# A hybrid encoder layer on one core: new order tables for TensorE, ScalarE, VectorE and GpSimd

## The chip, the core and the metric

The kernel runs on one core of one Trainium2 chip. The metric is the device time of one execution in microseconds (us), lower is better. Several executions are timed and their median is taken. One further execution is recorded by the hardware profiler, and all durations below come from that one.

In the rows, PE is TensorE (matmuls; PEld is its weight load), DVE is VectorE, ACT is ScalarE, POOL is GpSimd, and SP is SyncE. The letter q behind an engine means its queue: SPq rows are the DMAs that SP issues.

## What is computed

One layer of a streaming encoder, on 1024 prompt rows and 64 sample rows with a cache of 512 positions, all in fp32:

```python
def mixer_and_mlp(x):                      # x: (1024 + 64, 1024)
    z = x @ w_in                           # q, k, v and gate of FoX; u, v of the SGU; q, k, v of stick-breaking
    o_fox = softmax(q_f @ k_f.T / 8 + c_t - c_s) @ v_f        # 6 heads x 64, causal
    o_sgu = gelu(u) * (tril(w_s) @ layer_norm(gelu(v)) + b_s) # chunks of 128 positions, 4 groups x 64
    o_sb  = stick_breaking(q_s, k_s) @ v_s                    # 6 heads x 64, strictly causal
    o = rms_norm_per_head(concat(o_fox, o_sgu, o_sb)) * g_mix
    x = layer_norm(ALPHA * x + o @ w_out)
    h = relu(x @ w_up) ** 2                                   # 1024 -> 4096
    return layer_norm(ALPHA * x + h @ w_down)                 # 4096 -> 1024
```

The new rows of k, v, the forget gates and the SGU's v are outputs too.

## The kernel before

**Stages.** Everything is written once in Python, in a natural order, and then reordered. The mixer takes the first 600 us of the profiled execution: loads and transposes of x, the projections of k, v and q (`tok_mm`, L620 to L640), FoX, stick-breaking, the SGU's v and u (`sgu_v` L1052, `sgu_u` L1122), and the output product with its layer norm (`mix`, L483, and L440 to L530). Then comes `up` until about 958 us, `down` until 1295.3 us and a last layer norm of 10.5 us (the tail).

**Exactness.** A product of fp32 is made from three passes of a high and a low part (`PASSES`): for each operand ACT writes the high part and DVE or POOL the low part (`lo_sub`, L349 when the helper records it).

**Gelu in the SGU.** For each of nine row tiles t, `sgu_u` adds two halves of the product (tile `up`, L1137, DVE) and calls `gelu` (L1032): ACT squares into a tile `g1u` (L1033), DVE multiplies (L1034), ACT takes a sigmoid (L1035), POOL multiplies into a tile `sguu` (L1036), and SP stores `sguu` to DRAM (`u_dr`, L1143). `g1u` and `sguu` share one ring of three buffers (`tag="gl", bufs=3`). A tile that takes over the buffer of an earlier `sguu` has to wait until the store has read it. Which tile takes over from which is not written in the code: the pool hands out buffers in the order in which the ordered program frees them.

**The output mix** reads `o` back from DRAM (tiles `oo`), squares it on ACT (`sq`, L448), scales it on DVE (L455), transposes it on PE (`op`, L463), writes the result as high and low part (`oTb`, ACT L465 and DVE L349) and multiplies on PE into `mx` (L507). `ptssb`, `pthssb`, `ossb`, `ptnsb`, `ptnnsb` and `osbsb` are the last transposes, weights and outputs of the stick-breaking attention on the sample rows, which run beside it.

**Up.** The 4096 columns come in 16 pairs p. Each product of a 2 x 2 block is made with seven products of sums (`Chain`, L1572): a chain for s=0 (288 columns) and one for s=1 (256) each use four PSUM banks `zA`, `zB`, `zC`, `zD`, and a product is 12 matmuls (4 steps of depth by 3 passes, L1591). `zA` holds three products in turn; after each, ACT copies it out (`sn`, `sn`, `hh`, L1602), and the next product in that bank waits for the copy. The weights of pair p are loaded as `wr`; ACT and POOL make `wa` of them (L1529, L349), DVE makes sums in place (`w_sums`, L1538 to L1542), and ACT and DVE make `ws` of those (L1812, L349). DVE adds the products to `hh` (L1605 to L1611), squares the relu (L1623) and makes sums (L1632 to L1635); SP stores those (L1636 to L1640).

**Down.** `Down` (L2025) walks over groups g of 256 rows of h with accumulators A, B and D. The operands `h4a`, `h4b` and the weight parts `wd`, `b` are split the same way: ACT writes high parts (L1529, L1750), and `st` copies (L1754) help DVE to make low parts (L1755). The load buffers `hx`, `hr` and `awa` (DMAs at L1740, weights and accumulators at L1705 and L1766) are shared by several loads in turn.

**What sets the order.** Behind the body, `_build` takes the traced instructions of each engine and a table `ORDER[engine]` (L49 on). A word `n+k` means: n times, take the k-th of those that are left (0 is the next one as traced). Each instruction is tied to the one before it on its engine, so every engine runs exactly its table's order:

```python
        for word in ORDER[eng].split():
            n, k = (int(x or d) for x, d in zip(re.match(r"(\d*)\+?(\d*)", word).groups(), (1, 0)))
            for _ in range(n):
                i = left.pop(k)
                if prev is not None:
                    tc.add_manual_dep(i, prev.name, mybir.DependencyInfo(
```

The engines work their queues strictly in order, and waits between engines follow from the data. The table of SP orders all its DMAs.

Of the kernel before, what the change touches and what calls it, by code (L numbers as in the profile page):

```python
# [2446 lines left out]
```

## Time and profile before

| | before |
|---|---|
| median of 3 executions | 1312.68 us (1309.43 to 1313.89) |
| the profiled execution | 1307.53 us |
| its span (first to last instruction) | 1305.8 us |
| granted TensorE clock | 0.998 |
| PE busy | 1282.4 us, 98% of the span, 8851 matmuls |
| DVE, ACT, POOL busy | 958.9, 723.6, 609.3 us |

The profiled execution lies 5.2 us below the median and 1.9 us below the lowest of the timed ones. A row of the timeline reads: start, duration, engine, source line, operation, output and inputs, tile shape, count of equal instructions in a row, and in brackets how long the engine had been idle before it and what ended the idle time.

### The profile page before, as it was taken

The numbers are of one execution on the slowest core, as the hardware profiler recorded it, in microseconds if no ns is written. First come the engines' busy times: TensorE is split into PE (matmuls) and PEld (weight loads), VectorE is DVE, ScalarE is ACT, GpSimd is POOL, SyncE is SP. The second block draws the span as 40 slices with busy tenths as digits, with TensorE's granted clock in tenths as the row PEclk, the third lists the DMA queues.
The fourth block names the chain that finished last, engine by engine and source line by source line (L and its number), as shares of the span: only waits on it lengthen the run. The fifth ranks groups of instructions, "written<-read, shape, count | busy, mean of one in ns | idle before, by whom it ended". The sixth has DMA issues, their size and how long they took to land.

```text
span 1305.8 us, 24299 instructions
## 1 busy us (share of the span) xinstructions
PE 1282.4 (98%) x8851; PEld 1184.5 (91%) x8851; DVE 958.9 (73%) x1800; ACT 723.6 (55%) x1560; POOL 609.3 (47%) x670
## 2 busy tenths in 40 slices
PE   9999999999999999999999999999999999999996
PEld 9999999999989997878999999999988888888885
DVE  4678676677896587798877576766797767677777
ACT  4467666677675574343533222322368677667775
POOL 2232222356775576866322212121188666565557
PEclk9999999999999999999999999999999999999999
DMA  7445574232313358341333434434577344434433
GB/s 235 118 137 159 180 212 118 77 80 57 98 30 89 97 189 278 100 145 61 125 121 128 162 131 145 167 123 157 188 256 265 128 157 147 148 125 149 144 126 133
DMA packets 158048, 185.64 MB, mean 142 GB/s; under 512 B 27740, under 2 KB 116124, under 8 KB 157928
## 3 DMA queue, kind: packets, MB, share of 16 engines
q1 hardware_dynamic: 155832, 183.01, 43.6%
q8 instruction: 70, 1.15, 0.4%
q10 hardware_dynamic: 2096, 1.07, 0.3%
q14 instruction: 50, 0.41, 0.1%
HBM read 117.65 MB, written 60.10 MB: 136 GB/s over the span
## 4 chain that ended last, share of the span: by engine, by line
PE 47%; DVE 2%; DMA 1%; issue 0%; ACT 0%; SPq 0%; POOL 0%; DVEq 0%; ACTq 0%; POOLq 0%
PE A L2056 13%; PE zA L1591 10%; PE zD L1591 7%; PE D L2056 6%; PE zC L1591 3%; PE zB L1591 3%; PE B L2056 3%; PE ds L2102 1%; PE ds L2100 1%; PE lastD L2056 1%; DMA rd<-w_down 1%; PE lastB L2056 0%; DMA h_dr<-y 0%; DVE hh L1623 0%; DVE acc L2168 0%
## 5 line engine op out<-in xcount | busy, mean ns | idle before, releaser
L349 POOL TENSOR_TENSOR wa<-wr,wa 128x512 fp32r<-128x512 f32 x41 | 60.0, 1487 | 223.6 <-ACT wa L1529 223.4
L349 POOL TENSOR_TENSOR wd<-rd,wd 128x512 fp32r<-128x512 f32 x77 | 104.0, 1359 | 106.5 <-ACT wd L1529 105.2
L1591 PE MATMUL zD<-xo,ws 128*128 128x256 f32 (+1 forms) x720 | 141.9, 287 | 0.0
L1591 PE MATMUL zA<-xo,ws 128*128 128x288 f32 (+1 forms) x720 | 131.7, 288 | 1.1 <-ACT sn L1602 1.1
L1591 PEld LDWEIGHTS zD<-xo,ws 128*128 128x128 f32 x720 | 111.2, 188 | 0.2
L1591 PEld LDWEIGHTS zA<-xo,ws 128*128 128x128 f32 x720 | 107.2, 188 | 1.6 <-ACT sn L1602 1.6
L507 PE MATMUL mx<-xT,oTb 128*128 128x512 f32 (+1 forms) x416 | 107.3, 406 | 0.8 <-DVE y L512 0.8
L1602 ACT ACTIVATE sn<-zA 128x256 f32<-128x256 f32 (+1 forms) x80 | 31.1, 393 | 131.0 <-PE zA L1591 115.7
L635 PE MATMUL kvfox<-wkvfox,xT 128*128 128x256 f32 (+3 forms) x624 | 100.2, 294 | 0.8 <-ACT wkvfox L608 0.7
L635 PE MATMUL kvsb<-wkvsb,xT 128*128 128x256 f32 (+1 forms) x624 | 100.7, 291 | 0.0
L2056 PE MATMUL A<-wd,wd 128*128 128x512 f32 x312 | 93.6, 390 | 0.0
L507 PEld LDWEIGHTS mx<-xT,oTb 128*128 128x128 f32 (+1 forms) x416 | 74.0, 186 | 17.5 <-DVE y L512 1.0
L635 PEld LDWEIGHTS kvfox<-wkvfox,xT 128*128 128x128 f32 (+1 forms) x624 | 84.5, 187 | 1.6 <-ACT wkvfox L608 0.9
L635 PEld LDWEIGHTS kvsb<-wkvsb,xT 128*128 128x128 f32 (+1 forms) x624 | 84.6, 187 | 0.0
L1591 PE MATMUL zB<-xo,wa 128*128 128x288 f32 (+1 forms) x360 | 83.3, 287 | 0.0
L1591 PE MATMUL zC<-xo,wa 128*128 128x288 f32 (+1 forms) x360 | 82.4, 288 | 0.0
L1723 POOL TENSOR_TENSOR rd<-rd 128x512 f32<-128x512 f32 x56 | 74.3, 1327 | 13.2 <-DVE b L349 10.4
L821 POOL TENSOR_TENSOR sgsb<-sgsb,snsb 128x255 f32<-128x255 f32 (+7 forms) x48 | 58.2, 1213 | 45.2 <-DVE snsb L819 39.3
L2056 PE MATMUL A<-wd,h4a 128*128 128x512 f32 x240 | 77.4, 390 | 0.0
L1529 ACT ACTIVATE wd<-rd 128x512 fp32r<-128x512 f32 x105 | 63.3, 621 | 22.1 <-DMA rd<-w_down 10.2
L2023 DVE TENSOR_TENSOR acc<-acc,A 128x512 f32<-128x512 f32 x73 | 49.5, 683 | 29.8 <-PE A L2056 29.4
L819 DVE TENSOR_TENSOR_SCAN snsb<-snsb,one 128x256 f32<-128x256 f32 (+7 forms) x48 | 68.3, 1425 | 4.0 <-ACT snsb L818 3.2
(560 smaller groups left out, 3946.2 us busy)
## 6 DMA issues: line engine op xcount, KB each, us to landing
h_dr<-hh SPq DMA_DIRECT2D x30, 512.0 KB, 3.2
rd<-w_down SPq DMA_DIRECT2D x30, 512.0 KB, 4.4
wr<-w_up SPq DMA_DIRECT2D x13, 1024.0 KB, 5.8
hr<-h_dr SPq DMA_DIRECT2D x31, 384.0 KB, 3.1
h_dr<-hh SPq DMA_DIRECT2D x30, 384.0 KB, 3.9
raw<-w_in SPq DMA_DIRECT2D x44, 256.0 KB, 3.2
wo_dr<-swo SPq DMA_DIRECT2D x32, 256.0 KB, 2.3
xT<-wo_dr SPq DMA_DIRECT2D x8, 1024.0 KB, 8.0
```

The lines of the kernel that those rows point to most:

```text
L349: eng.tensor_tensor(out, src, hi.bitcast(F32), op=ALU.subtract)
L507: nc.tensor.matmul(acc[0:m], oT[:, k, hx, 0:m], wo[k // 4][hw][:, k % 4, cs], start=(i == 0), stop=(i == len(seq) - 1))
L635: nc.tensor.matmul(acc[0:n, c0:c0 + n1 - n0], xT[k // 4][:, k % 4, c:c + n], wt[:, k, hw, n0:n1], start=(i == 0), stop=(i == len(seq) - 1))
L819: nc.vector.tensor_tensor_scan(g[:, 0:n][:, ::-1], g[:, 0:n][:, ::-1], one.broadcast_to([P, n]), 1.0, op0=ALU.mult, op1=ALU.bypass)
L821: nc.gpsimd.tensor_tensor(s[:, 0:n - 1], s[:, 0:n - 1], g[:, 1:n], op=ALU.mult)
L1529: nc.scalar.activation(hi, raw, AF.Copy)
L1591: nc.tensor.matmul(z, w[:, hw, k], xop(s, bo, hx)[:, k, :], start=(new and k == 0 and j == 0), stop=(k == 3 and j == 2), skip_group_check= ...
L1602: nc.scalar.activation(c, z, AF.Copy)
L1723: eng.tensor_tensor(r[:, o], r[:, x], r[:, y], op=ALU.subtract)
L2023: nc.vector.tensor_tensor(out, out if other is None else other, bank, op=ALU.add)
L2056: nc.tensor.matmul(z, h[:, hx, q, o], wset[self.c % 2][q][:, hw, wb], start=((n in (0, 3) or n == 1 and self.c == 0) and q == 0 and j == 0 ...
L2100: nc.tensor.matmul(z, hs[:, q, f].rearrange("p h c -> p (h c)"), w[:, 0], start=(q == 0 and f == 0), stop=False, skip_group_check=True)
```

## The change

Only the four tables `ORDER["PE"]`, `ORDER["ACT"]`, `ORDER["DVE"]` and `ORDER["POOL"]` are new. `ORDER["SP"]`, every line of code and every instruction are as before: 8851 matmuls on PE, and the same 1502, 1701 and 656 ordered instructions on ACT, DVE and POOL. The author's planner, which wrote the tables, took a DMA's landing time from the bytes that are outstanding when it is issued, and was made to keep the products of one accumulator of `up` together. The tables take 40 lines less in all, so a line of code has a number that is 40 lower after the change: L1033 is L993, L349 is L309.

```diff
 ORDER["ACT"] = """
-3 +3 2+5 1 +1 1 2+3 +4 +2 +7 +3 +6 +2 +6 1 +9 2+1 +3 3 +3 +4 +8 1 +1 +2 +5 2 +2 2+6 5 2+5 1 +2 +3 1 2+12 +1 +3
+2 +7 +4 +6 4 2+3 2+4 +2 +6 +2 1 +4 1 +4 1 +7 +3 3 +6 +5 +3 +7 +2 2 +4 1 +7 1 +6 +1 4 +5 +1 +2 1 +3 2+13 +1 +4
...
```

Most instructions move by some 10 to 30 places. Three places follow. `[waits ...]` names what an instruction waits for: an engine's semaphore, or a DMA's (DMAHW and a number).

**The opening of the output mix, ACT.** Here the last gelus of the SGU's u (`g1u6`, `g1u7`: row tiles 6 and 7) run among the last pieces of the stick-breaking attention of the sample rows. Before:

```order
L851 ACTIVATE pthsb2_3_1_3_7822<-ptsb2_3_1_3_7818 128x384 [waits DVE_49,PE_49]
L1035 ACTIVATE g1u6_7710<-g1u6_7710 128x256 [waits DVE_49]
L448 ACTIVATE sq1_7616<-oo1_1_7614 128x512 [waits DMAHW2_49,Activation_49,Pool_49]
L851 ACTIVATE pthssb2_7849<-ptssb2_7844 128x512 [waits PE_49]
L906 ACTIVATE osbsb2_3_1_7837<-osb2_3_1_7725 128x256 [waits PE_49]
L1033 ACTIVATE g1u7_7757<-up6_7261 128x256 [waits Pool_49]
L851 ACTIVATE ptnnsb2_7854<-ptnsb2_7852 128x128 [waits DVE_49]
L1035 ACTIVATE g1u7_7757<-g1u7_7757 128x256 [waits DVE_49]
```

After:

```order
L811 ACTIVATE pthsb2_3_1_3_7822<-ptsb2_3_1_3_7818 128x384 [waits PE_49,Activation_49]
L993 ACTIVATE g1u6_7710<-up6_7261 128x256 [waits DMAHW4_49]
L408 ACTIVATE sq1_7616<-oo1_1_7614 128x512 [waits DVE_49,DMAHW2_49,Activation_49,Pool_49]
L995 ACTIVATE g1u6_7710<-g1u6_7710 128x256 [waits DVE_49]
L811 ACTIVATE pthssb2_7849<-ptssb2_7844 128x512 [waits PE_49]
L993 ACTIVATE g1u7_7757<-up6_7261 128x256 [waits DMAHW1_49,Pool_49]
L811 ACTIVATE ptnnsb2_7854<-ptnsb2_7852 128x128 [waits Activation_49]
L995 ACTIVATE g1u7_7757<-g1u7_7757 128x256 [waits DVE_49]
L866 ACTIVATE osbsb2_3_1_7837<-osb2_3_1_7725 128x256
```

`g1u7` moved ahead of `osbsb2_3_1`, and `ptnnsb2` stays behind it. Its wait changed too: it took over a buffer from `g1u6` before, and takes over that of `sguu5` now, so it waits for the store of `sguu5` (DMAHW1 in this row). `g1u6` in the same way now waits for a store, that of `sguu4`.

On DVE at the same place, before:

```order
L349 TENSOR_TENSOR pthssb2_7849<-ptssb2_7844,pthssb2_7849 128x512 [waits Activation_49]
L455 TENSOR_TENSOR oo1_0_7613<-oo1_0_7613,ss1_7618 128x512 [waits DMAHW1_49,Pool_49]
L1034 SCALAR_TENSOR_TENSOR g1u7_7757<-g1u7_7757,up6_7261 128x256 [waits Activation_49]
L349 TENSOR_TENSOR ptnnsb2_7854<-ptnsb2_7852,ptnnsb2_7854 128x128 [waits PE_49,Activation_49]
L450 TENSOR_REDUCE ss1_7618<-sq1_7616 128x8
L1034 SCALAR_TENSOR_TENSOR g1u8_7775<-g1u8_7775,up8_7292 64x256 [waits DMAHW4_49,DMAHW3_49,Activation_49]
L451 SCALAR_TENSOR_TENSOR ss1_7618<-ss1_7618,rge_7590 128x8 [waits DVE_49]
```

After:

```order
L309 TENSOR_TENSOR ptnnsb2_7854<-ptnsb2_7852,ptnnsb2_7854 128x128 [waits DVE_49,PE_49,Activation_49]
L411 SCALAR_TENSOR_TENSOR ss1_7618<-ss1_7618,rge_7590 128x8 [waits DVE_49]
L994 SCALAR_TENSOR_TENSOR g1u7_7757<-g1u7_7757,up6_7261 128x256 [waits DMAHW1_49,Pool_49]
L415 TENSOR_TENSOR oo1_0_7613<-oo1_0_7613,ss1_7618 128x512 [waits Pool_49]
L309 TENSOR_TENSOR pthssb2_7849<-ptssb2_7844,pthssb2_7849 128x512 [waits PE_49]
L875 TENSOR_REDUCE otsb2_3_0_7734<-otpsb2_3_0_7735 128x2x64 [waits DMAHW5_49]
```

`ptnnsb2` and `g1u7`, which need ACT's results of the same names, moved ahead of `oo1_0` (the next tile of the mix) and of `pthssb2`.

**Up, p=8.** ACT copies out `zA8_0` and `zA8_1` and makes `ws9`. Before:

```order
L1529 ACTIVATE wa9_10778<-wr9_10776 128x512 x2
L1602 ACTIVATE sn8_0_10793<-zA8_0_10797 128x288 [waits DVE_49,PE_49,Activation_49]
L1602 ACTIVATE sn8_0_10793<-zA8_0_10797 128x288 [waits PE_49]
L1602 ACTIVATE sn8_1_10795<-zA8_1_10811 128x256 [waits DVE_49,PE_49,Activation_49]
L1812 ACTIVATE ws9_10789<-wr9_10776 128x1024 [waits DVE_49] x2
L1602 ACTIVATE sn8_1_10795<-zA8_1_10811 128x256 [waits PE_49]
L1602 ACTIVATE hh8_0_10794<-zA8_0_10797 128x288 [waits DMAHW2_49,DMAHW1_49,DMAHW3_49,DVE_49,PE_49]
L1602 ACTIVATE sn8_1_10795<-zA8_1_10811 128x256 [waits PE_49]
```

After:

```order
L1489 ACTIVATE wa9_10778<-wr9_10776 128x512 x2
L1562 ACTIVATE sn8_0_10793<-zA8_0_10797 128x288 [waits DVE_49,PE_49,Activation_49]
L1562 ACTIVATE sn8_1_10795<-zA8_1_10811 128x256 [waits DVE_49,Activation_49]
L1772 ACTIVATE ws9_10789<-wr9_10776 128x1024 [waits DVE_49,PE_49]
L1772 ACTIVATE ws9_10789<-wr9_10776 128x1024
L1562 ACTIVATE sn8_0_10793<-zA8_0_10797 128x288 [waits PE_49]
L1562 ACTIVATE sn8_1_10795<-zA8_1_10811 128x256
L1562 ACTIVATE hh8_0_10794<-zA8_0_10797 128x288 [waits DMAHW2_49,DMAHW1_49,DMAHW3_49,DVE_49,PE_49]
L1562 ACTIVATE sn8_1_10795<-zA8_1_10811 128x256 [waits PE_49]
```

The two halves of `ws9` now stand ahead of the second copies of both banks, where they stood between or behind them. On DVE, between the sums of `wr9` that `ws9` needs, before:

```order
L1538 TENSOR_TENSOR wr9_10776<-wr9_10776 128x4x128 [waits DMAHW0_49,Pool_49]
L1539 TENSOR_TENSOR wr9_10776<-wr9_10776 128x4x128 [waits DVE_49]
L1632 TENSOR_TENSOR hh7_0_10568<-hh7_0_10568 128x256
L1541 TENSOR_TENSOR wr9_10776<-wr9_10776 128x4x128 [waits DVE_49]
L1623 SCALAR_TENSOR_TENSOR hh7_1_10570<-hh7_1_10570 128x1024
L1542 TENSOR_TENSOR wr9_10776<-wr9_10776 128x4x128 [waits DVE_49]
```

After:

```order
L1498 TENSOR_TENSOR wr9_10776<-wr9_10776 128x4x128 [waits DMAHW0_49,Activation_49,Pool_49]
L1595 TENSOR_TENSOR hh7_0_10568<-hh7_0_10568 128x256 [waits DVE_49]
L1583 SCALAR_TENSOR_TENSOR hh7_1_10570<-hh7_1_10570 128x1024 [waits DVE_49]
L1592 TENSOR_TENSOR hh7_0_10568<-hh7_0_10568 128x256
L1593 TENSOR_TENSOR hh7_0_10568<-hh7_0_10568 128x256 [waits DVE_49]
L1499 TENSOR_TENSOR wr9_10776<-wr9_10776 128x4x128
L1592 TENSOR_TENSOR hh7_1_10570<-hh7_1_10570 128x256
L1501 TENSOR_TENSOR wr9_10776<-wr9_10776 128x4x128 [waits DVE_49,Activation_49]
L1593 TENSOR_TENSOR hh7_1_10570<-hh7_1_10570 128x256 [waits DVE_49]
L1502 TENSOR_TENSOR wr9_10776<-wr9_10776 128x4x128 [waits DVE_49]
```

Four more instructions on `hh7` stand between the first and the last sum than before. On PE the third product of `zA8_0`, which needs the second copy, has 37 more matmuls ahead of it (11 of `zA8_1`, 9 of `zD8_0`, 7 each of `zB8_0` and `zD8_1`, 5 of `zB8_1`, less 2 of `zC8_0`), and all products stand in runs of up to 12.

**Down, group 1, ACT.** `h4b` is the operand that PE's first products of the group need; its second half comes from the load buffer `awa`, which held weights before (`wd0_1<-awa`). Before:

```order
L2073 ACTIVATE p10_0_12654<-A0_0_12640 128x512 [waits PE_49]
L1529 ACTIVATE wd0_1_12494<-awa_12374 128x512 [waits DVE_49]
L2073 ACTIVATE p10_1_12656<-A0_1_12647 128x512 [waits PE_49]
L1750 ACTIVATE h4b_12629<-hx_12375 128x512 [waits DMAHW5_49]
L1754 ACTIVATE st9_12712<-h4b_12629 128x512 [waits DVE_49,Activation_49]
L1750 ACTIVATE h4a_12369<-hx_12375 128x512 [waits PE_49]
L1754 ACTIVATE st11_12769<-h4a_12369 128x512 [waits DVE_49,Activation_49]
L1529 ACTIVATE b12_1_12628<-rb0_1_12839 128x512 [waits DMAHW0_49]
L1529 ACTIVATE b12_0_12626<-rb0_0_12835 128x512 [waits DMAHW7_49]
L1529 ACTIVATE wd1_0_12625<-rd1_0_12733 128x512 [waits DMAHW3_49,Pool_49]
L1750 ACTIVATE h4b_12629<-awa_12374 128x512 [waits DMAHW2_49]
```

After:

```order
L1489 ACTIVATE wd0_0_12493<-rd0_0_12296 128x512
L1710 ACTIVATE h4b_12629<-hx_12375 128x512 [waits DMAHW5_49]
L1489 ACTIVATE wd0_1_12494<-awa_12374 128x512
L1710 ACTIVATE h4a_12369<-hx_12375 128x512 [waits PE_49]
L1489 ACTIVATE b12_0_12626<-rb0_0_12835 128x512 [waits DMAHW7_49]
L1714 ACTIVATE st9_12712<-h4b_12629 128x512 [waits DVE_49,Activation_49]
L1714 ACTIVATE st11_12769<-h4a_12369 128x512 [waits DVE_49]
L1489 ACTIVATE b12_1_12628<-rb0_1_12839 128x512 [waits DMAHW0_49]
L1710 ACTIVATE wd0_0_12493<-hr1_0_12693 128x384 [waits DMAHW6_49,PE_49]
L1710 ACTIVATE h4b_12629<-awa_12374 128x512 [waits DMAHW2_49]
L1714 ACTIVATE st10_12752<-h4b_12629 128x512 [waits Activation_49]
L1489 ACTIVATE wd1_0_12625<-rd1_0_12733 128x512 [waits DMAHW3_49,Pool_49]
```

The second half of `h4b` now stands ahead of `wd1_0<-rd1_0` instead of behind it. The last `wd0_1<-awa`, after which the buffer can be loaded again, moved from ahead of the first half of `h4b` to behind it.

414 rows, old and new, of the table ORDER are left out of this document.

## The prediction

> **What bounds the kernel now.** I read the page's busy times first, then the waits of PE, then the timeline at the places where PE waits or where the new tables change what stands ahead of what.
>
> ```profile
> span 1305.8 us, 24299 instructions
> PE 1282.4 (98%) x8851; PEld 1184.5 (91%) x8851; DVE 958.9 (73%) x1800; ACT 723.6 (55%) x1560; POOL 609.3 (47%) x670
> ```
>
> PE is busy in all but 23.4 us of the span, and the same 8851 matmuls run in either order. The waits of PE, longest first, and PE's last row:
>
> ```profile
> PE warm L1370 <- POOL ident masks.py:199: 1.6, 1, 1.6
> PE zA L1591 <- ACT sn L1602: 1.1, 2, 0.6
> PE otpfox L914 <- DVE kpfox L349: 0.9, 1, 0.9
> PE mx L507 <- DVE y L512: 0.8, 1, 0.8
> ...
> PE A L2056 <- ACT h4b L1750: 0.7, 1, 0.7
> ...
> PE sgu L635 <- DVE up L1137: 0.5, 1, 0.5
> ```
>
> ```profile
> 1293.77 1.52 PE L2056 MATMUL A<-wd,wd 128*128 128x512 f32 x6
> ```
>
> PE ends at 1295.3 and the span at 1305.8, so 10.5 of the 23.4 us are the tail behind PE, 1.6 are the start, and 11.3 are small waits, none above 0.9. That is all a reordering of PE's suppliers can win. What it can lose has no such limit: each engine runs its queue strictly in order, and PE can't make up a wait later.
>
> **Part one, what goes.** In up, PE waits twice behind ACT:
>
> ```profile
> 651.84 0.38 ACT L1602 ACTIVATE sn<-zA 128x256 f32<-128x256 f32 x1 [2.35 <-DMA h_dr<-y]
> 652.28 0.62 PE L1591 MATMUL zA<-xo,ws 128*128 128x256 f32 x3 [0.59 <-ACT sn L1602]
> ```
>
> ```profile
> 759.09 1.06 ACT L1812 ACTIVATE ws<-wr 128x1024 fp32r<-128x1024 f32 x1 [0.87 <-DVE wr L1542]
> 760.05 0.67 ACT L1602 ACTIVATE sn<-zA 128x288 f32<-128x288 f32 x2
> 760.50 0.40 PE L1591 MATMUL zA<-xo,ws 128*128 128x288 f32 x1 [0.56 <-ACT sn L1602]
> ```
>
> In the new PE table the products that wait here start later by over 1 us of PE work, so both waits go: -1.2. In FoX the wait of `otpfox` goes, since DVE's work on `kpfox` stands earlier: -0.9. At the end of the SGU's u the wait of `sgu` for `up` goes (0.5), and two of `osb` behind it get 0.1 later each: -0.3. `mx` for `y` gets 0.1 us more room against a wait of 0.8: -0.1. In the tail two pieces of VectorE work of the last layer norm move ahead of PE's last evacuations; I take -0.5, between 0 and the 1.4 of two pieces of 128x512 (0.68 each at 509.94 below). Keeping the products of one accumulator together saves nothing that I can read: runs of one accumulator step at the same pace as mixed rows.
>
> ```profile
> 793.86 0.86 PE L1591 MATMUL zA<-xo,wa 128*128 128x256 f32 x6
> 756.60 1.61 PE L1591 MATMUL zA<-xo,ws 128*128 128x288 f32 x11
> ```
>
> A lone matmul's row shows about 0.28 us, so the runs step at (0.86 - 0.28) / 5 = 0.116 and (1.61 - 0.29) / 10 = 0.132 us; I take -0.3 for fewer changes, between 0 and -1. Sum of what goes: -3.3.
>
> **Part two, the mix opening.** Before, the stores of `sguu` hold POOL, and nobody waits for that:
>
> ```profile
> 503.55 0.32 SPq L1143 DMA_DIRECT2D u_dr<-sguu  x1
> 513.17 0.73 POOL L1036 TENSOR_TENSOR sguu<-g1u,up 128x256 f32<-128x256 f32 x1 [1.95 <-DMA u_dr<-sguu]
> ```
>
> ```profile
> 500.89 0.42 DVE L1034 SCALAR_TENSOR_TENSOR g1u<-g1u,up 128x256 f32<-128x256 f32 x1
> 505.16 0.67 DVE L450 TENSOR_REDUCE ss<-sq 128x8 f32<-128x512 f32 x1
> 509.94 0.68 DVE L455 TENSOR_TENSOR oo<-oo,ss 128x512 f32<-128x512 f32 x1
> 511.25 0.42 ACT L1033 ACTIVATE g1u<-up 128x256 f32<-128x256 f32 x1 [1.68 <-POOL sguu L1036]
> 511.58 0.26 ACT L851 ACTIVATE ptnnsb<-ptnsb 128x128 fp32r<-128x128 f32 x1
> 511.39 0.27 PE L463 MATMUL op<-ident,oo 128*128 128x128 f32 x1
> 508.96 2.00 PE L507 MATMUL mx<-xT,oTb 128*128 128x512 f32 x8
> ```
>
> The store of `sguu5` is issued at 503.55, and the tile that takes over its buffer starts at 513.17: 9.6 us. After the change ACT's `g1u7` takes over that buffer. The store itself comes later: DVE's `g1u5` stood at 500.89 and now stands behind the low part of `oTb`, whose successor started at 505.16, so that is its earliest time; from `g1u5` to the issue took 2.66 us, so the issue moves to 507.8. If the store lands when the queue clears, as before at 513.2, `g1u7` starts then, `ptnnsb` 0.33 later (511.25 to 511.58), DVE's part of it 0.46 behind that, then the sums and `g1u7` (0.65) and `oo1_0` (0.68): 515.3. PE needs `oo1_0` for the transposes that ran at 511.39. Its new table has 14 matmuls of 512 columns more ahead of them and one of 256 less, at (2.00 - 0.40) / 7 = 0.229 and 0.11 us each: 3.1, so at 514.5. PE waits 0.8, and 0.6 more for `pthssb`, which DVE now makes behind `oo1_0`: 1.4. If the store takes 9.6 us from its new issue, all is 4.2 later: 5.6. If it takes as little as the 2.1 us below, nothing waits: 0.
>
> ```profile
> uu<-u_dr SPq DMA_DIRECT2D x3, 128.0 KB, 2.1
> ```
>
> I take +2.8, the middle between the ends: the store joins the same loads as before, but later. The Trainium skill, DMA: Bandwidth & Descriptors, section "Anatomy of one DMA — SWDGE (gpsimd) path", puts a DMA at about 2.0 us and 1 us per 436 KB, which for 128 KB would be an estimate of 2.3 us: by that rule this term is 0. The trace disagrees here with 9.6 us, though the quiet row of 2.1 us agrees.
>
> **Part three, up at p=8.** After the change both halves of `ws9` stand on ACT ahead of the second copy of `zA8_0`, which is the order that cost PE 0.56 at 760.50 in p=6.
>
> ```profile
> 795.32 0.68 DVE L1538 TENSOR_TENSOR wr<-wr 128x512 f32<-128x512 f32 x1
> 798.72 0.68 DVE L1542 TENSOR_TENSOR wr<-wr 128x512 f32<-128x512 f32 x1
> 799.65 0.75 DVE L1633 TENSOR_TENSOR hh<-hh 128x256 f32<-128x256 f32 x2
> 799.43 1.06 ACT L1812 ACTIVATE ws<-wr 128x1024 fp32r<-128x1024 f32 x1 [0.60 <-DVE wr L1542]
> 798.35 1.02 PE L1591 MATMUL zA<-xo,ws 128*128 128x288 f32 x7
> ```
>
> The last sum ended at 799.4. Four more pieces of `hh` of 0.35 to 0.42 stand ahead of it: 800.9. Two halves of `ws9` at 1.0 and the copy at 0.4 end at 803.3. PE's third product began at 798.35; 37 more matmuls stand ahead (23 of 0.116, 14 of 0.132): 4.5, so 802.85. PE waits 0.5. The same order in p=7 makes `ws8` and so the load of `wr9` up to 1.5 later, and then it is 2.0. I take +1.5, and for p=7, 9 and 15, whose tables mix `ws`, `sn` and `hh` alike, +0.5 each (the 0.56 of p=6), between 0 and 3 together.
>
> **Part four, down's group 1.** Before, ACT waits for a weight load, and behind it stands `h4b`:
>
> ```profile
> 963.11 0.62 ACT L1529 ACTIVATE wd<-awa 128x512 fp32r<-128x512 f32 x1
> 964.04 4.11 POOL L349 TENSOR_TENSOR wd<-awa,wd 128x512 fp32r<-128x512 f32 x2
> 963.79 0.32 SPq L1740 DMA_DIRECT2D hx<-h_dr  x1
> 968.95 0.63 ACT L1750 ACTIVATE h4b<-hx 128x512 fp32r<-128x512 f32 x1 [4.00 <-DMA hx<-h_dr]
> 970.19 0.38 SPq L1740 DMA_DIRECT2D awa<-h_dr  x1
> 977.26 0.63 ACT L1529 ACTIVATE wd<-rd 128x512 fp32r<-128x512 f32 x1 [1.40 <-DMA rd<-w_down]
> 977.79 0.61 ACT L1750 ACTIVATE h4b<-awa 128x512 fp32r<-128x512 f32 x1
> 978.46 0.50 PE L2056 MATMUL A<-wd,h4b 128*128 128x512 f32 x1 [0.71 <-ACT h4b L1750]
> ```
>
> The change takes `h4b` from behind that load, but puts the last reader of `awa` behind the wait for `hx`: it runs at 969.5 instead of 963.11, POOL's half takes 1.3 to 2.05 behind it, so the load of `awa` is issued at 971.5 to 972.2 instead of 970.19. With the 5.1 us of `hx` (963.79 to 968.95) it lands at 976.6 to 977.3, and `h4b` is ready at 977.2 to 977.9. PE wants it at 977.5 (0.2 earlier than before): a wait of 0 to 0.4 in place of 0.7. If DVE's new order holds the load of `hx` as well, as its work on `wd0_1` now stands up to 1.2 later, the wait is 1.6. Net -0.7 to +0.9; I take +0.8, because `h4a` and the first accumulators wait in the same chain.
>
> **Part five, the rest.** The stretch of the SGU's v is the tightest for DVE, and the new table loads ACT and DVE in it a little later:
>
> ```profile
> 340.00:400.00 60.00, 57.57 (x465) 54.88 (x464) 53.70 (x101) 40.86 (x102) 48.18 (x54) 1.00 0.19 47
> ```
>
> DVE is busy 53.7 of 60 us there. I take +0.5 (0 to 1), +0.2 for the head, whose first split waits for a later load, and +0.5 for the later groups of down, where no row shows a wait now (0 to 2). Sum of what comes: 2.8 + 1.5 + 1.5 + 0.8 + 0.5 + 0.2 + 0.5 = 7.8. Net 7.8 - 3.3 = +4.5 us, from 1307.5 to 1312.0 in a profiled execution. The median of the timed executions lies 5.2 above the profiled one, so 1312.7 + 4.5 = 1317.2. I can tell about 0.3%, 3.9 us, from no change.
>
> **The rivals.** First, not slower but faster: the new landings are right, the store of `sguu5` lands within 3 us, and the waits of parts three to five stay below 0.1 as before. Then only what goes counts, with the 0.7 of `h4b`: -4.0, 1308.7. For it: the quiet 2.1 us, and no row of before shows PE late in p=8. Against it: 9.6 us at that very place. It decides at a landing of 511.8, 1.4 us ahead of before's. By the page's 2.3 us alone, with the other parts as forecast, the time would be 1314.4. Second, no difference: half of the new waits fall on slack (the store at its lower 1.4, p=8 at 0.5, the rest at half), +3.6 against -3.3: 1313.0. For it speaks that PE is 98% busy and each place moves by tenths. Third, worse: the store takes its 9.6 us and the late loads of up and down all take their upper ends (5.6 + 2.0 + 3 + 0.9 + 3.2): 14.7 - 3.3, 1324.1.
>
> **How the numbers follow.** Forecast 45%, no difference 28%, faster 20%, worse 7%. The forecast's own range is 1314 to 1321; two in three of its cases lie beyond 3.9 us, which with the worst makes slower 0.38. The faster rival lies just beyond the bound: 0.20. The rest, 0.42, is no difference, so slower and same are nearly even, and the sign of the forecast is not sure. The range runs from 1308 (the faster rival) to 1324 (the worst).
>
> **What would show it.** In the profile after: no wait of `zA` near 651 and 760; ACT's `g1u` of row tile 7 idle for a DMA `u_dr<-sguu`, and `op` on PE released late by DVE's `oo` near 513; `zA` waiting for `sn` near 802; `A` for `h4b` near 977, with ACT released by the DMA of `awa` instead of `rd`. It is wrong if `g1u` starts before 512 or if PE's waits sum to less than before's.

## The result, and the profile after

The kernel after takes 1304.28 us in the median (6 runs, 1302.47 to 1307.09), the one before 1311.37 beside it (6 runs, 1309.43 to 1313.89). The ratio is 0.9945 with a 95% interval of 0.9929 to 0.9961: faster by 0.55%. Forecast were 1317.2.

The head of the page after (span; busy time of each engine, its share of the span, its instructions), and then PE's waits (what PE did next and in which line, what ended the wait; us in total, times, the longest):

```profile
span 1303.0 us, 24347 instructions
PE 1276.9 (98%) x8851; PEld 1180.1 (91%) x8851; DVE 964.4 (74%) x1800; ACT 721.5 (55%) x1560; POOL 606.2 (47%) x670
```

```profile
PE sgv L595 <- DVE sgvv L996: 1.5, 3, 1.0
PE sgm L1043 <- ACT so L1047: 1.2, 1, 1.2
PE mx L467 <- ACT oTb L425: 1.2, 1, 1.2
PE zA L1551 <- ACT sn L1562: 1.1, 3, 0.5
PE Ssb L795 <- ACT snsb L778: 1.1, 2, 0.7
PE zD L1551 <- DVE hh L1565: 0.9, 2, 0.6
PE A L2016 <- DVE acc L1981: 0.8, 1, 0.8
```

The profiled execution took 1304.70 us against 1307.53. PE's busy time fell by 5.5 us, from 1282.4 to 1276.9, for the same 8851 matmuls at the same granted clock (0.998 and 0.997). Between its matmuls PE idled 14.5 us instead of 11.3. So the waits grew by 3.2, as forecast in direction, and the kernel is faster because PE's own matmuls take less time. That was not in the forecast.

The two profiled executions differ by 2.8 us, the medians by 7.1, since before's profiled one was a low one. Before was profiled once more, unchanged (`before_again`): 1310.52 us, PE busy 1283.6, idle 13.1.

**Where the time came from.** I compared the executions at points where PE has done the same matmuls. After is 0.8 us ahead at 149 us, 2.4 at 165 (the wait of `otpfox` is gone), and then slowly 4.1 at 336. Of these 1.7 us waits make 0.2: the time that PE spends on the same matmuls (number 1329 to 2810) without its idle time falls from 175.4 to 173.9. After loses 3.0 at the opening of the mix (511 to 526) and gets 1.2 back by 565, as `mx` no longer waits at 557. In up the lead grows slowly from 2.9 to 5.3, and the time without idle there falls from 333.8 to 331.7; at down's opening it loses about 2. The slow parts show also as counts of matmuls in a fixed window. The first number behind "PE busy" in such a row is its busy time, the x its matmuls; before, before a second time, after:

```profile
205.00:335.00 130.00, 129.93 (x1112) 129.46 (x1111) 93.14 (x195) 89.76 (x221) 59.96 (x97) 1.00 0.31 85
760.00:940.00 180.00, 179.50 (x1441) 179.50 (x1442) 123.19 (x197) 49.72 (x94) 34.78 (x24) 1.00 0.45 150
```

```profile
205.00:335.00 130.00, 129.93 (x1111) 129.46 (x1110) 93.14 (x194) 89.57 (x220) 60.45 (x97) 1.00 0.31 84
```

```profile
205.00:335.00 130.00, 129.93 (x1124) 129.36 (x1123) 94.32 (x200) 89.57 (x224) 64.13 (x98) 1.00 0.31 85
760.00:940.00 180.00, 180.00 (x1461) 180.00 (x1460) 124.89 (x202) 50.55 (x96) 32.94 (x25) 1.00 0.45 152
```

PE is busy for the whole of the 130 us in all three, at a full clock, and gets through 12 to 13 matmuls more. (The two kernels don't have the very same matmuls in such a window, so the times above, over the same matmuls, are the measure of the gain.) Busy time in such a row isn't the measure of work; the count beside it is.

### The profile page after: what moved, and what is told of

It reads as the page before. It is cut to its first block, busy times and chain, and to the rows that moved or that the text cites. A ratio compares the mean times of both kernels' runs of the same rounds, so it can differ in the third digit from the quotient of the medians.

```text
span 1303.0 us, 24347 instructions
## 1 busy us (share of the span) xinstructions
PE 1276.9 (98%) x8851; PEld 1180.1 (91%) x8851; DVE 964.4 (74%) x1800; ACT 721.5 (55%) x1560; POOL 606.2 (47%) x670
## 3 DMA queue, kind: packets, MB, share of 16 engines
q8 instruction: 70, 1.15, 0.4%
## 5 line engine op out<-in xcount | busy, mean ns | idle before, releaser
L309 POOL TENSOR_TENSOR wa<-wr,wa 128x512 fp32r<-128x512 f32 x41 | 58.2, 1443 | 226.9 <-ACT wa L1489 226.9
L309 POOL TENSOR_TENSOR wd<-rd,wd 128x512 fp32r<-128x512 f32 x77 | 102.6, 1343 | 110.5 <-ACT wd L1489 96.8
L1551 PE MATMUL zD<-xo,ws 128*128 128x288 f32 (+1 forms) x720 | 116.6, 287 | 0.9 <-DVE hh L1565 0.9
L1551 PE MATMUL zA<-xo,ws 128*128 128x256 f32 (+1 forms) x720 | 110.5, 287 | 1.1 <-ACT sn L1562 1.1
L1551 PEld LDWEIGHTS zD<-xo,ws 128*128 128x128 f32 x720 | 100.4, 188 | 1.7 <-DVE hh L1565 1.4
L1551 PEld LDWEIGHTS zA<-xo,ws 128*128 128x128 f32 x720 | 97.8, 188 | 1.8 <-ACT sn L1562 1.8
L1562 ACT ACTIVATE sn<-zA 128x288 f32<-128x288 f32 (+1 forms) x80 | 30.6, 391 | 114.0 <-PE zA L1551 75.2
L595 PE MATMUL kvsb<-wkvsb,xT 128*128 128x256 f32 (+1 forms) x624 | 81.2, 281 | 0.0
L781 POOL TENSOR_TENSOR sgsb<-sgsb,snsb 128x127 f32<-128x127 f32 (+7 forms) x48 | 60.3, 1259 | 36.7 <-DVE snsb L779 32.3
L1983 DVE TENSOR_TENSOR acc<-acc,A 128x512 f32<-128x512 f32 x73 | 49.5, 684 | 32.7 <-PE A L2016 32.3
L779 DVE TENSOR_TENSOR_SCAN snsb<-snsb,one 128x128 f32<-128x128 f32 (+7 forms) x48 | 66.4, 1388 | 7.6 <-ACT snsb L778 6.2
L2016 PEld LDWEIGHTS A<-wd,wd 128*128 128x128 f32 x312 | 58.6, 188 | 13.0
L1551 PE MATMUL zB<-xo,wa 128*128 128x288 f32 (+1 forms) x360 | 61.5, 287 | 0.0
```

Source lines behind the costliest of these rows:

```text
L309: eng.tensor_tensor(out, src, hi.bitcast(F32), op=ALU.subtract)
L595: nc.tensor.matmul(acc[0:n, c0:c0 + n1 - n0], xT[k // 4][:, k % 4, c:c + n], wt[:, k, hw, n0:n1], start=(i == 0), stop=(i == len(seq) - 1))
L779: nc.vector.tensor_tensor_scan(g[:, 0:n][:, ::-1], g[:, 0:n][:, ::-1], one.broadcast_to([P, n]), 1.0, op0=ALU.mult, op1=ALU.bypass)
L781: nc.gpsimd.tensor_tensor(s[:, 0:n - 1], s[:, 0:n - 1], g[:, 1:n], op=ALU.mult)
L1551: nc.tensor.matmul(z, w[:, hw, k], xop(s, bo, hx)[:, k, :], start=(new and k == 0 and j == 0), stop=(k == 3 and j == 2), skip_group_check= ...
L1562: nc.scalar.activation(c, z, AF.Copy)
```

## The experiments

Two theories were put against each other. **Pace**: PE's matmuls take less time in the new order, by their sequence alone. **Waits**: the gain is that of waits that went, and the rest is scatter. All times stand against before's median in the same group of runs (1309.1 to 1311.4).

**Mixing the widths of up's products again.** In up, before changes between 256 and 288 columns 890 times, after 237 times. This kernel deals out after's matmuls between two waits in turn by width, at most 32 at a time (1119 changes; accumulators change 1491 times, in after 772). In outline:

```diff
-PE, up: zA 256 x10, zD 256 x8, zB 288 x15
+PE, up: zA 256, zB 288, zD 256, zB 288, zA 256, ...
```

> The changed kernel with one edit: in up, PE's matmuls between two waits are dealt out in turn by width, so that the column count changes 1119 times in up instead of 237 (before: 890) and the accumulator 1491 times instead of 772 (before: 1529). All other engines keep the new tables. Theory (pace): a 256-column matmul steps at 118 ns while widths alternate and at about 115 in a long run of 256, so up's 1300 matmuls of 256 columns cost 2 ns more each: up longer by 2 to 3 us in the profile, time 1306 to 1308 against 1304.3 of the changed kernel. Rival (only the other engines' tables and the waits matter): no change, 1304.3 within 1.5.

Measured: 1314.21 (ratio 1.003, 1.0018 to 1.0042). All of the gain is gone and more. A step of 256 columns takes 116.84 ns in place of 115.48 (before 117.12), 1.8 us over up; but most of the loss is new waits for ACT and DVE in up, some 7 us. Products end later there, which would explain them; that was not taken apart.

**Mixing only the accumulators.** The widths stay in runs, the accumulators alternate (209 changes of width, 1158 of accumulator). In outline:

```diff
-PE, up: zA 256 x6, zD 256 x6
+PE, up: zA 256, zD 256, zA 256, zD 256, ...
```

> The changed kernel with PE's matmuls of up reordered between waits so that runs of one width stay (209 changes of width instead of 237) but the accumulators inside a run alternate (1158 changes of accumulator instead of 772). Theory (pace follows the width): no change of the step, 115 to 116 ns at 256 columns, 1304.3 within 1.5. Rival (pace follows the accumulator, as the change's words have it): about half of the way back to before's 117 ns, up longer by 1 to 1.5 us.

Measured: 1303.66 (ratio 0.9953, 0.994 to 0.9966), a step of 115.38 ns. What the change says it does, keeping the products of one accumulator together, is not what makes the pace. With the run before, this points to the runs of one width that come with it.

**The other way round.** Before, with up's matmuls sorted by width between two waits, at most 16 at a time (362 changes of width). In outline:

```diff
-PE, up: 256 x2, 288 x2, 256, 288 x3, ...
+PE, up: 256 x3, 288 x5, ...
```

> The kernel before with one edit: in up, PE's matmuls between two waits (at most 16) are sorted by width, so that the width changes 362 times instead of 890 and the accumulator 1351 times instead of 1529. Theory (pace): the 256-column matmuls fall from 117 to about 115.5 ns a step, up shorter by 1.5 to 2 us; waits of up may grow by some tenths, since products end up to 1.5 us later. Rival (accumulators): 0.3 us at most. Rival (waits only): no change or slower.

Measured: 1314.42 (ratio 1.0032, 1.0021 to 1.0042), slower by 4 us where a gain was expected. The step did shorten (116.17 ns, 1.3 us over up), but the waits for ACT and DVE in up grew by more (some 4 us). Sorting for pace did not pay here without suppliers that are planned with it.

**The stream of matmuls alone, made up.** Nothing but 2160 matmuls on resident data, in nine sections of different runs; all the rest is left out. In outline:

```diff
+for n, c in pattern:            # (256, 12) or (288, 12) or (256, 1), (288, 1) ...
+    for i in range(c):
+        nc.tensor.matmul(bank[:, 0:n], w[next], m[next])
```

> Everything of the reference is left out; only streams of matmuls of the same kind as up's run, with nothing to wait for, in sections: 256 columns in runs of 12 per accumulator, 288 in runs of 12, both in turn by 12, by 4, by 2 and by 1, then 256 with another accumulator at each matmul, and 256 with a 128-column matmul every 12th or every third. Theory (width): about 115 ns a step in long runs of 256, also with changing accumulators, and about 118 for the first four 256 behind a change of width, so the average of the 256s is 116 when changing by 12 and 118 by 4, 2 and 1; 288 stays at 132 everywhere. Rival (accumulators): 115 only where an accumulator keeps for 12, 118 where it changes at each matmul. Rival (a fixed cost of other engines' traffic in the real kernel): no difference between the sections.

Measured: 256 columns step at 118.2 to 119.9 ns in the mean of every section, 288 at 131.5 to 132.5. The sections with the longest runs were not the fastest, and changing accumulators made no difference of note. This spoke against both theories' mechanism: a made-up stream doesn't show the shortening, so it takes something of the kernel's own sequence of weights and rows, which the next two runs took.

**The kernels' own matmuls alone.** The 1481 matmuls of the mixer (from number 1329) and the 2675 of up, in before's and after's order, with the same addresses of weights and moving rows, and all other work left out. In the first of the two runs all products wrote into the first bank of PSUM, not into the banks that its text speaks of; the second has the true banks, and variants of the order. In outline:

```diff
+for w, m, bank, n in rows_of(kernel):       # before's or after's PE table, one stretch
+    nc.tensor.matmul(bank[:, 0:n], mem[:, w:w + 128], mem[:, m:m + n])
```

> TensorE's matmuls alone, everything else left out: matmuls 1329 to 2810 (mixer) and 4662 to 7337 (up) of both orders, with the widths, the places of the weights, of the moving rows and of the accumulators that they have in the two kernels, back to back on resident data, in the sequence mixer before, mixer after, up before, up after, mixer after, mixer before. Theory (the order of TensorE's own matmuls sets its pace): mixer after is 1.5 to 2 us shorter than mixer before, both times, and up after about 2 us shorter than up before. Rival (the pace comes from what the other engines do meanwhile, or from waits too short for a row): each pair agrees within 0.3 us.

Measured, from the first matmul's start to the last one's: mixer 173.58 before, 171.69 and 171.71 after; up 332.97 before, 331.50 after. (The first section waited for its data and doesn't count.)

> TensorE's matmuls alone again, now with each product in the bank of its accumulator (in the run before, all wrote into the first bank). The sequence: mixer before twice (the first one waits for the data), mixer after, mixer before with the transposes gathered and mixer after with them spread (each within every 24 matmuls), up before, up after, up before sorted by width, up after with widths mixed evenly, up after with accumulators in turn but widths sorted (each within every 24). Theory (a step gets shorter in long runs of one width, and accumulators cost nothing): up after 1.3 to 1.6 us below up before, up before sorted like up after within 0.4, up after mixed 0.5 to 2 above up before, accumulators in turn like up after within 0.4; mixer after 1.9 below mixer before, gathered 1 to 2 below mixer before, spread 1 to 2 above mixer after. Rival (the accumulator decides): sorted by width stays like up before, accumulators in turn becomes like up before or worse, and gathering transposes moves nothing.

The sections as windows, in this order: mixer before, mixer after, before with transposes gathered, after with transposes spread; up before, up after, before sorted by width, after with widths mixed, after with accumulators in turn:

```profile
178.87:352.44 173.57, 173.57 (x1483) 173.45 (x1482) 0.00 (x0) 3.02 (x9) 0.00 (x0) 1.00 0.00 1
352.44:524.09 171.65, 171.65 (x1482) 171.62 (x1482) 0.00 (x0) 3.21 (x9) 0.00 (x0) 1.00 0.00 1
524.09:697.29 173.20, 173.20 (x1483) 172.99 (x1482) 0.00 (x0) 2.91 (x9) 0.00 (x0) 1.00 0.00 1
697.29:871.17 173.88, 173.88 (x1482) 173.79 (x1482) 0.00 (x0) 3.36 (x9) 0.00 (x0) 1.00 0.00 1
871.17:1204.24 333.07, 333.07 (x2677) 332.92 (x2676) 0.00 (x0) 2.78 (x9) 0.00 (x0) 1.00 0.00 1
1204.24:1535.71 331.47, 331.47 (x2676) 331.39 (x2676) 0.00 (x0) 4.20 (x11) 0.00 (x0) 1.00 0.00 1
1535.71:1867.79 332.08, 332.08 (x2678) 332.06 (x2676) 0.00 (x0) 2.14 (x6) 0.00 (x0) 1.00 0.00 1
1867.79:2201.64 333.85, 333.85 (x2676) 333.76 (x2675) 0.00 (x0) 4.01 (x11) 0.00 (x0) 1.00 0.00 1
2201.64:2533.33 331.69, 331.69 (x2677) 331.54 (x2675) 0.00 (x0) 2.69 (x7) 0.00 (x0) 1.00 0.00 1
```

The second number is the length of a section, and PE is busy in all of it. The mixer's new order is 1.9 us shorter and up's 1.6, with next to nothing else at work (ACT's few copies are 2 to 4 us of a section). So PE's own order makes these gains, whatever its suppliers do. What in the order makes them is shown in part. In up, mixing the widths of after's costs 2.4, accumulators in turn cost 0.2, and sorting before's by width brings 1.0 of the 1.6, where all but 0.4 was expected: though the width then changes as seldom as in after, 0.6 is left over and stays open. In the mixer, spreading the transposes among the products costs 2.2, but gathering before's gains only 0.4 where 1 to 2 were expected. Longer runs aren't the rest: before with transposes gathered changes its width less often (310 times) than after (376), and changes less often between transposes and products (124 against 278), and is still 1.6 us longer. What makes most of the mixer's 1.9 stays open. In the section of up after, the step of 256 columns by its place in a run of one width is 117.9, 117.1, 117.2, 116.2, 115.3, 115.4 and, from the seventh on, 115.5 ns.

**Which part of the tables gains.** Six kernels take one set of tables up to a point and the other behind it. In outline:

```diff
-ORDER = before
+ORDER = first[:t] + [i for i in second if i not in first[:t]]   # per engine; t: what the first's profile had started by then
```

> The old tables up to 615 us (mixer and output product), the new ones for up, down and the tail. If the profile pair is read as it stands, the new rest is worth nothing in sum (up -2.7, down +1.9, tail -0.5 in the two profiles: -1.3), so 1309 against 1310.3 of before. The theory says that pace gives 2.2 of that in up and that the waits of down take it back. Rival (the gain that the profiles don't show, 6 against 2.8, lies in up and down): 1306 to 1307.

> The new tables up to 612 us, the old ones behind. From the profile pair the mixer is worth 3.0 us, so 1307.3 against 1310.3. If the gain of the medians lies in the mixer: 1305. If it lies in up and down: 1309 to 1310. With the other half the two should add up to the 6 to 7 us of the whole change.

> The new tables up to 200 us, the old order for what is left of it behind. Theory (the gain is spread over the mixer, and each part keeps what it won): the 2.2 us that after is ahead at 200 us stay, ratio 0.9983, about 1308.2 against 1310.4. Rival (what a part wins early is given back at the next place where an engine or a load is late anyway): ratio 0.9995 to 1.0005.

> The new tables up to 352 us, the old order behind. Theory (spread, and each part keeps what it won): the 4.0 us that after is ahead there stay, ratio 0.9969, about 1306.3. Rival (the 1.9 us between 200 and 345 us, where no wait of TensorE reaches 0.1 us, are the profiled execution's own and not the order's): as with the new tables to 200 us, 0.9983, 1308.2.

> The new tables up to the end of up (946 us), the old ones for down. Theory (the parts add up: mixer -5, up -2.5, and down's new order costs 2 to 3): ratio 0.9935 to 0.9945, about 1302.5 to 1303, 1 to 2 us below after. Rival (down's loss of 2.2 us at 950 to 1000 us comes with the earlier end of up, since its first weights land when they land): ratio as after's, 0.995 to 0.996.

> The old tables up to the end of up (951.5 us), the new ones for down. Theory (down's new opening costs by itself what the profiles show at 950 to 1000 us): 2 to 3 us slower than before, ratio 1.0015 to 1.0023. Rival (down's loss in after comes with the earlier end of up, as its first weights land when they land): ratio 0.9995 to 1.0005.

| kernel | median us | ratio to before (95%) |
|---|---|---|
| old mixer, new rest | 1307.99 | 0.9981 (0.9973 to 0.999) |
| new mixer, old rest | 1304.70 | 0.9958 (0.9946 to 0.997) |
| new to 200 us, old rest | 1314.59 | 1.0035 (1.0023 to 1.0047) |
| new to 345 us, old rest | 1310.11 | 1.0007 (0.9998 to 1.0015) |
| new to the end of up, old down | 1302.50 | 0.9947 (0.9933 to 0.996) |
| old to the end of up, new down | 1311.09 | 1.0015 (1.0006 to 1.0024) |

The mixer gains 0.42%, as the reading that the gain of the medians lies in the mixer had it (1305). Up and down together gain 0.19%, which lies between what its theory and its rival said (1309; 1306 to 1307). Together that is 0.61% beside the 0.55% of the whole. Behind the old up, down's new order costs 0.15%, 2.0 us, which its theory said and the rival (that it follows from up's earlier end) didn't. Behind the new up it shows no cost: new tables with the old down came out at after's own ratio, where 0.9935 to 0.9945 were expected. The two runs don't agree, so what down's order costs in after isn't settled, nor is a version that beats after shown.

The two early cuts missed both their theories, and why is worth a look. The pace followed the tables: with the new ones to 200 us the window of 205 to 335 us, in the old order again, holds 1109 matmuls (before 1111 and 1112), with the new ones to 345 us 1127 (after 1124). So the gain between 200 and 345 us is the order's, and not one execution's own.

```profile
205.00:335.00 130.00, 129.93 (x1109) 129.31 (x1108) 93.06 (x192) 89.59 (x220) 59.91 (x97) 1.00 0.30 83
```

```profile
205.00:335.00 130.00, 129.93 (x1127) 129.44 (x1126) 94.43 (x200) 89.64 (x224) 64.10 (x98) 1.00 0.31 86
```

With the tables to 345 us, PE began up at 614.1 us, 4 ahead of before. All of that was lost between 646 and 652. ACT's first copy `sn` of pair 1, s=0, waited there for three DMAs and DVE; in before it waits for PE alone, and the wait for the others stands two copies later, at s=1. In the order's rows, the cut kernel and then before:

```
L1582 ACTIVATE sn1_0_9193<-zA1_0_9195 128x288 [waits DMAHW6_49,DMAHW4_49,DMAHW7_49,DVE_49,PE_49]
...
L1602 ACTIVATE sn1_0_9193<-zA1_0_9195 128x288 [waits PE_49]
```

The timeline below puts the end of this wait down to DVE's sums, but those that the copy needs ended at 643.97. What came last is a store of pair 0's sums (`h_dr<-y`), issued at 643.52: it landed at 646.14, and the copy starts at 646.29. The buffers are handed out in the order in which all engines free them. `sn1_0` lies at the same place in both kernels, but what lay there before it is another tile: in the cut kernel `y3`, the sums of pair 0 that this store reads, in before the weights `w0_1`. Every instruction behind 352 us is in the old order all the same. New to 345 us, timeline of ACT and PE, and then windows around it (the number behind POOL's is the granted clock):

```profile
646.29 0.41 ACT L1582 ACTIVATE sn<-zA 128x288 f32<-128x288 f32 x1 [8.00 <-DVE h L1615]
646.76 1.09 PE L1571 MATMUL zA<-xo,ws 128*128 128x288 f32 x3 [4.63 <-ACT sn L1582]
652.01 0.30 PE L1571 MATMUL zC<-xo,wa 128*128 128x288 f32 x1
```

```profile
636.00:641.00 5.00, 5.00 (x44) 5.00 (x43) 5.00 (x10) 1.74 (x3) 0.00 (x0) 1.00 0.02 3
646.70:648.70 2.00, 1.94 (x8) 1.95 (x9) 0.00 (x0) 0.00 (x1) 0.00 (x0) 0.50 1.00 294
648.70:650.70 2.00, 2.00 (x10) 2.00 (x9) 0.00 (x0) 0.00 (x0) 0.00 (x0) 0.50 0.97 258
651.40:653.40 2.00, 2.00 (x18) 2.00 (x17) 0.00 (x0) 0.41 (x1) 0.00 (x0) 0.98 1.05 324
```

The wait is 4.63 us, and behind it the granted clock is 0.50 until about 651.4: 8 to 10 matmuls in 2 us instead of 18. From matmul 4662 to 5000 this kernel takes 49.5 us, before 43.3: 4.0 more of wait (4.63 against 0.59) and some 2.2 of half clock. With the tables to 200 us PE waited 2.42 and 0.78 at 659 to 660, with the half clock behind; where these waits come from was not worked out.

**The opening of the mix.** After, with `osbsb2_3_1` ahead of `g1u7` on ACT, and `pthssb2` and `oo1_0` ahead of `ptnnsb2` on DVE:

```diff
-ACT: g1u7 (L993), ptnnsb2 (L811), g1u7 (L995), osbsb2_3_1 (L866)
+ACT: osbsb2_3_1 (L866), g1u7 (L993), ptnnsb2 (L811), g1u7 (L995)
-DVE: ptnnsb2, ss1, g1u7, oo1_0, pthssb2
+DVE: pthssb2, oo1_0, ptnnsb2, ss1, g1u7
```

> The changed kernel with three instructions moved back at the opening of the mix: on ACT osbsb2_3_1 ahead of g1u7, on DVE pthssb2 and oo1_0 ahead of ptnnsb2. The wait of g1u7 for the store of sguu5 stays. Theory (the store's wait reaches PE through those three): the wait of op at 511 (0.7) goes and PE's later rows move up by 0.8 to 1.4, time 1303 to 1303.5. Rival (the wait is only passed on): mx waits longer for oTb at 520.9 (1.2 now), no change of the time.

Measured: 1303.59 (ratio 0.9946, 0.993 to 0.9962). The wait of `op` at 511 us is gone, that of `mx` behind it grew from 1.16 to 1.44 us, and the time is after's. The times alone can't tell 0.8 us (the interval is some 2 us wide each way), but the profiles do: matmuls 3250 to 4240 take 135.0 us in both kernels, so the wait was passed on and the rival was right. The loss there sits in the chain of the whole opening, not in one wait.

## Why the prediction was wrong

The step that failed stands in part one: "Keeping the products of one accumulator together saves nothing that I can read: runs of one accumulator step at the same pace as mixed rows", at -0.3. It was read from two groups of before, both within a run of one width, so that they could not show what a change of width costs; and it was asked of up only. PE's own order made 1.6 us in up and 1.9 in the mixer when taken alone, 3.5 together; in place, the same matmuls without PE's idle time take 2.2 and 1.5 us less. That is the larger part of the 5.5 us by which PE's busy time fell, and about half of the 7.1 between the medians. The two stretches hold 4156 of the 8851 matmuls; no run took the others alone. The quoted sentence itself holds for accumulators (alternating them costs 0.2 alone); the step that failed is that it stood for all that PE's order could win. Since only waits were counted ("That is all a reordering of PE's suppliers can win"), the faster rival's end was put at -4.0 in all.

**Part one, the waits.** Right for `otpfox`: it is gone, as is the wait of `zA` for `sn` at 760. At 651 a wait stays, 0.53 in place of 0.59, with the same cause as before: ACT, which made `wa` late, behind a wait for the store `h_dr<-y`:

```profile
649.05 1.15 ACT L1489 ACTIVATE wa<-wr 128x512 fp32r<-128x512 f32 x2 [2.55 <-DMA h_dr<-y]
650.11 0.36 ACT L1562 ACTIVATE sn<-zA 128x256 f32<-128x256 f32 x1
650.53 0.62 PE L1551 MATMUL zA<-xo,ws 128*128 128x256 f32 x3 [0.53 <-ACT sn L1562]
```

`mx` for `y` at 557 was costed at -0.1; the whole 0.8 went, and 1.2 us with the work around it. Two new waits came, 0.27 of `zD` at 655 and 0.21 of `zA` at 735, so that up's waits sum to 1.0 instead of 1.15: next to none of up's gain is waits. The tail is 10.0 instead of 10.5, as taken. `sgu` with `osb` gave nothing: 1.64 us of waits against 1.69.

**Part two, the mix opening.** After, PE, ACT, DVE and SP at that place, and how long the DMAs on `u_dr`, stores and loads together, took to land from 480 to 520 us:

```profile
501.16 0.41 DVE L994 SCALAR_TENSOR_TENSOR g1u<-g1u,up 128x256 f32<-128x256 f32 x1
502.92 0.32 SPq L1103 DMA_DIRECT2D u_dr<-sguu  x1
506.40 0.42 ACT L993 ACTIVATE g1u<-up 128x256 f32<-128x256 f32 x1 [3.95 <-DMA u_dr<-sguu]
509.34 0.42 ACT L993 ACTIVATE g1u<-up 128x256 f32<-128x256 f32 x1 [1.12 <-DMA u_dr<-sguu]
511.31 0.33 PE L423 MATMUL op<-ident,oo 128*128 128x128 f32 x1 [0.70 <-DVE oo L415]
520.94 0.73 PE L467 MATMUL mx<-xT,oTb 128*128 128x512 f32 x2 [1.16 <-ACT oTb L425]
...
DMA to landing us min/median/max: 1.7/3.1/8.5
```

The mechanism is as forecast: `g1u7` waits for the store of `sguu5`, and `op` waits for `oo` behind it, 0.70 us (0.8 in the working). Both ends of the working were off. DVE's `g1u5` ran at 501.16 and not behind 505.16, so the store was issued at 502.92 instead of 507.8 and landed 6.4 us later, at 509.3. That is before the 511.8 from which the faster rival should have held; but PE wanted the tile at 510.6 instead of 514.5, as it was ahead by then, so the wait came all the same. ACT's longer wait is the one ahead of it, 3.95 us of `g1u6` for the store of `sguu4`.

Between 511 and 526 us the change loses 3.0 (forecast 2.8), but that the two are close is partly luck. By 516 us only 1.3 have gone on the path of the forecast, `op` for `oo`. 1.9 go from 519 to 524, where `mx` waits for `oTb`: ACT makes it behind a `sq` for which it was idle 5.52 us, waiting for POOL's `oo`. In before ACT made that `oTb` later still, at 521.97, but PE came later too. 1.2 of the loss come back by 565.

The rule of the Trainium skill, DMA: Bandwidth & Descriptors, section "Anatomy of one DMA — SWDGE (gpsimd) path", from which an estimate of 2.3 us for this store was worked out, is fitted on DMAs that GpSimd issues, and this one is SP's. Here 6.4 us were measured, and 1.7 to 8.5 for the four stores of 128 KB to `u_dr` from 480 to 520 us whose landing the trace has.

**Part three, up at p=8** and p=7, 9 and 15: +3.0 forecast, nothing came.

```profile
796.08 2.01 ACT L1772 ACTIVATE ws<-wr 128x1024 fp32r<-128x1024 f32 x2 [5.12 <-DVE wr L1502]
797.99 0.66 ACT L1562 ACTIVATE sn<-zA 128x288 f32<-128x288 f32 x2
798.72 3.11 PE L1551 MATMUL zA<-xo,ws 128*128 128x288 f32 x24
```

Both halves of `ws9` do stand ahead of `sn`, as read from the order. But they could start at 796.08; the working had DVE's last sum at 800.9 by setting the moved pieces onto before's clock, as if the new row began no earlier than the old. It began at 790.55 us instead of 795.32, and DVE's last sum ended at 795.30 instead of 798.72. PE's `zA` doesn't wait.

**Part four, down's opening:** +0.8 forecast, and +0.5 for the later groups; 2.0 measured by the new down behind the old up, and about 2 lost here between the two profiles. The sign was right there, but new tables with the old down show no cost. The waits are not that of `A` for `h4b`: one is for DVE's addition into `awa`, the other for an addition that itself waits for its accumulator's load (PE, PE, DVE):

```profile
972.80 0.70 PE L2016 MATMUL A<-wd,h4a 128*128 128x512 f32 x2 [0.45 <-DVE awa L1983]
986.32 0.96 PE L2016 MATMUL A<-wd 128*128 128x512 f32 x3 [0.77 <-DVE acc L1981]
985.58 0.69 DVE L1981 SCALAR_TENSOR_TENSOR acc<-acc,A 128x512 f32<-128x512 f32 x1 [0.78 <-DMA acc<-x_dr]
```

Ahead of these, `zA` and `zD` wait 0.37 and 0.62 at 949 and 953, at the last pair of up.

**Part five.** The stretch of the SGU's v: +0.5 forecast. From 345 to 400 us PE's waits of 0.15 and more sum to 3.14 us (the longest 1.24 and 1.01) instead of 2.09 (0.60 and 0.47), so +1.0. Behind it, at 446, `Ssb` waits 0.71 for ACT's `snsb`, which no part of the prediction has.

**The sum.** Between the two profiled executions +4.5 was forecast and -2.8 came, a difference of 7.3. By stretches of the same matmuls (us that after gains; a minus is a loss):

| stretch | forecast | measured |
|---|---|---|
| to 167 us | 0.7 | 2.4 |
| 167 to 341 | 0 | 1.7 |
| 341 to 500 | -0.2 | 0.3 |
| 500 to 526 | -2.8 | -3.4 |
| 526 to 618 | 0.1 | 1.9 |
| up, 618 to 945 | -1.5 | 2.4 |
| 945 to PE's end | -1.3 | -3.0 |
| tail | 0.5 | 0.5 |

The largest miss is up, 3.9: there 3.0 us of waits were forecast for part three that didn't come, and PE's time without idle, put at 0.3 less, fell by 2.2. From 167 to 341 us, where nothing was forecast, it fell by 1.5. Of the 2.4 to 167 us, 0.8 came by 149 us, where PE's waits sum to 1.6 us in both kernels, and the rest with `otpfox`. The loss of part two had about the right size, and 945 to the end cost more than twice its sum.

The step from the profiled execution to the median, +5.2 in the working, was wrong for after, whose profiled execution lies at its median (1304.70 and 1304.28). What makes the executions of one kernel differ by 4 us stays open; between before's two profiles 1.4 us arise by the end of the mixer and 1.9 between 988 and 999 us, where the second has waits of 0.72 and 0.60 that the first has not.

Open is also why a step of 256 columns shortens along a run of one width, when a made-up stream of long runs steps at 118 to 120 ns throughout; what makes the 0.6 of up's 1.6 that sorting by width doesn't bring; and what makes most of the mixer's 1.9.

## What to carry to other kernels

When PE is 98% busy, the waits bound what its suppliers can win, but not what its own order can: take the time of the same matmuls in both profiles without PE's idle time, count matmuls in equal windows, and time PE's own sequence alone. Mixing widths and spreading transposes among products each cost over 2 us here. Cost a moved instruction against the new timeline, where what stands ahead of it has moved too; set on the old clock, it gives waits that don't come. And two orders can't be joined in the middle without a look at the buffers: which tile lay in one before follows from all that was freed earlier.

## What the runs showed of the hardware

The wait of 4.63 us cost more than itself. With the new tables to 345 us, PE's last matmul ends at 642.13; the granted clock fell at 644.66, 2.5 us into the wait, and stayed at 0.50 for 6.8 us, 4.7 of them behind the wait:

```profile
642.20:644.60 2.40, 0.00 (x0) 0.00 (x0) 2.37 (x6) 0.00 (x0) 0.00 (x0) 1.00 0.12 48
644.70:646.70 2.00, 0.00 (x0) 0.00 (x0) 1.15 (x3) 0.41 (x1) 0.00 (x0) 0.50 0.99 382
```

Waits of 2.42 and 0.78 us, with 0.67 of work between, lowered the clock too, for 3.4 us (new tables to 200 us):

```profile
658.90:660.90 2.00, 1.13 (x5) 0.90 (x6) 2.00 (x4) 0.04 (x1) 2.00 (x2) 0.86 0.00 0
660.90:662.90 2.00, 2.00 (x10) 2.00 (x10) 1.97 (x4) 0.00 (x0) 0.25 (x1) 0.50 0.03 8
662.90:664.90 2.00, 2.00 (x14) 2.00 (x14) 0.74 (x2) 0.91 (x2) 0.00 (x0) 0.79 0.00 0
```

PE does 10 matmuls in 2 us at 0.50 and 14 at 0.79. The Trainium skill, TensorE: Matmul & The Clock Gate, section "Part 1: The HAM clock gate (the "warmup" mystery)", has the clock halved after an idle window of about 3.4 us and released after as much of work. Here it fell sooner, 2.5 us into one wait and behind two of 2.42 and 0.78; half the clock lasted 3.4 us in one kernel, as the page has it, and 4.7 of work in the other.

A matmul's step depends a little on what stands beside it. Alone on resident data, 256 columns step at 117.9 ns first in a run of one width and at 115.5 from the seventh on, in the sequence of up after; a made-up stream did not show this.
